# Broadcasting the gain rows and the mLSTM gate maxima by way of DRAM instead of by matmuls

## The chip, the cores and the metric

The kernel runs on one core of a Trainium2 chip. The metric is the device time of one execution in microseconds (us); shown are the median, the lowest and the highest of three runs. A profile is a separate execution, recorded instruction by instruction. TensorE (PE) does the matmuls, VectorE (DVE), ScalarE (ACT) and GpSimd (POOL) the elementwise work. SyncE (SP) issues every DMA of this kernel, from one queue and in order. The granted clock (PEclk) is the share of full speed that TensorE was allowed.

## The reference

Two blocks on 256 tokens of 1024 features in float32. The first block (two layers of feed-forward and a convolution and recurrence mixer) is hardly touched. The second is a two-layer network with adaptive norms, on 256 tokens `x` and 256 context tokens `ctx`. What the change concerns is this:

```python
def adaln(cond, w_mod, b_mod):                      # cond: one vector for x, one for ctx
    m = silu(cond) @ w_mod + b_mod                  # [3 * 1024]
    return split(m, 3)                              # shift, scale, gain "ga"

h = rms_norm(x, g_pre) * (1 + sc) + sh
x = x + ga * rms_norm(mixer(h), g_post)             # layer 0: hyena + attention; layer 1: mLSTM

# mLSTM of layer 1, 8 heads, two directions, chunk form, with running maxima m_row:
s   = (q @ k.T) * exp(d - m_row)                    # d from the cumulated log-gates
num = s @ v + ...; den = sum(s) + ...
h   = num / maximum(abs(den), exp(-m_row))
```

## The kernel before

All float32 products are made of three matmuls of 12-bit halves (`mm3`, L125 to L129). `wload` (L99) brings 1 MB of weights into `raw` (two buffers), and ACT (L96) and DVE (L97) split it into high and low halves `wh`, `wl` (three chunks of buffers). PSUM, the matmuls' output memory, has eight banks: two tagged `mm`, two `tp` (transposes and small products), four `acc`. The program is written as generators that are woven into each other; the tile framework fixes the order on each engine when the kernel is built, and on the chip each engine runs its list strictly in that order.

**The modulation** (`modulation`, L518) makes the vector `silu(cond) @ w_mod` of a layer without matmuls. For each of 24 column blocks a step loads 512 KB of `w_mod` into `mraw` (L534) and DVE multiplies and sums it with the condition, once for `x` and once for `ctx` (L537). So a step has two such DVE operations; of layer 1 the last eight steps have one. Behind the last step the biases are added (L544 to L547). In the Hyena stage of layer 0, `mods` is the modulation of layer 1. There `mraw` has a single buffer (`bufs` is 1), so the load of a step can only start when the DVE operations of the step before are done.

**The Hyena stage** takes 1024 channels in four groups g of 256. `project(g)` does eight groups of 24 matmuls `mm<-HT` (128x512; the text calls them HT groups), each followed by a short convolution on ACT and DVE (L682 to L684). `convolve(g)` transposes the gated input `gg` (L997), multiplies with DFT tables `dft` (`acc<-gT`), takes the product with the filter `F` (DVE, L1015 to L1017), goes back (`acc<-dft,Y`) and gates the result into `hyo`; `rows(g)` multiplies it with output weights. The order in the program is:

```python
mods = modulation(pool, 1, range(12), 1)
weave(hy.project(0), mods, 2)
for g in range(1, 4):
    weave(hy.project(g), paired(chain(hy.convolve(g - 1), *([hy.rows(g - 1)] if g < 3 else [])), mods))
run(mods)
```

`weave` issues a step of `mods` after each two of `project(0)` and then what is left of it, so in the program's text all of `mods` stands ahead of `convolve(0)`; where its instructions land on each engine is the framework's choice.

**The gain rows** (`gain_rows`, L549) put `sqrt(1024) * ga * g_post`, held feature by feature over partitions in `mod`, into a tile `gb` of 1024 columns that is the same on all 128 partitions. Per half, DVE makes a diagonal block `dg` (L553), PE multiplies it by ones (L558) into a `tp` bank, and ACT scales it out (L559). It is called three times, for (layer, condition) = (0,0), (0,1) and (1,0), each shortly ahead of the use of `gb` in `postnorm` (L651).

**The mLSTM.** `mlstm_gates` leaves the running maxima of all heads as `R` [8, 384] per direction and splits them into high and low halves `gRs` (L1113, L1114). `head(h)` needs row h on all 128 partitions: two matmuls with a selector `sel` [8, 128] (L1211, L1220) put it into a `tp` bank; from there DVE adds the mask (`rm`, L1222) and ACT takes the exponentials (L1226). At the end of each head a norm weight `hn` is loaded, broadcast by the DMA (L1252).

Of the kernel before, what the change touches and what calls it, by code (L numbers as in the profile page):

```python
# [9 lines left out]
F32 = mybir.dt.float32  # L10
# [7 lines left out]
P = 128  # L18
D = 1024
# [14 lines left out]
def weave(main, side, n=1):  # L34
    """Issue main, with a step of side after every n steps of it, then what is left of side."""
    side = iter(side)
    for i, _ in enumerate(main):
        if i % n == n - 1:
            next(side, None)
    for _ in side:  # L40
        pass
# [8 lines left out]
def paired(*gens):  # L50
    """The steps of the first, each with one of the others."""
    gens = [iter(g) for g in gens]
    first = gens[0]
    for _ in first:
        for g in gens[1:]:
            next(g, None)
        yield
# [8 lines left out]
def body(ctx: ExitStack, tc: tile.TileContext, a: dict, out: bass.AP):  # L66
# [27 lines left out]
    def split(h, l, src, eng=V):  # L94
        """src = h + l, exactly; h has 12 significant bits, l the other 12."""
        S.copy(h, src)  # L96
        eng.tensor_tensor(l, src, h.bitcast(F32), op=ALU.subtract)  # L97

    def wload(src, parts=1, aside=False):  # L99
        """A [128, 2048] chunk of weights, in two halves (high part, low part)."""  # L100
# [15 lines left out]
    def rsqrt(dst, var, eps, n, scale=1.0):  # L116
        """dst = 1 / sqrt(scale * var + eps)"""
        vv = sp.tile([P, n], F32, tag=f"rs{n}", name="rsv", bufs=2)
        G.tensor_scalar(vv, var, scale, eps, op0=ALU.mult, op1=ALU.add)  # L119
        G.tensor_tensor(dst, vv, mhalf[:, :n], op=ALU.pow)  # L120
# [4 lines left out]
    def mm3(p, lh, ll, rh, rl, first, last):  # L125
        """p += (lh + ll).T @ (rh + rl)"""
# [4 lines left out]
    def agroup(p, w, lhs):  # L131
        """p [128 tok, 512] = sum over kt of lhs(kt).T @ w, w halves of [2 kt x 512]."""
# [7 lines left out]
    def btile(p, w, rhs):  # L140
        """p [128 features, tokens] = sum over kt of w[kt].T @ rhs(kt), w a list of (high, low) [128, 128]."""
        for kt, (wh, wl) in enumerate(w):
            mm3(p, wh, wl, *rhs(kt), kt == 0, kt == len(w) - 1)

    def bcols(w, j):
        """The [128, 128] blocks of feature tile j of a [8 kt x 256] chunk."""
        return [(h[:, k * 256 + j * P :][:, :P], l[:, k * 256 + j * P :][:, :P]) for h, l in w for k in range(4)]

    def rows_acc(chunks, lhs, nch, side=iter(())):
        """Token tiles of [tok, 1024], each in two banks; chunk c of [2 kt x 1024]; the first tile is done early."""  # L150
# [26 lines left out]
    def transposed(blocks):  # L177
        """The transposes of [128, 128] blocks, in one bank."""
# [5 lines left out]
    # ---------------------------------------------------------------- small vectors  # L184
# [14 lines left out]
    def exp_dve(dst, x, t):  # L199
        """exp(x) for x <= 0 by range reduction and a polynomial."""  # L200
# [16 lines left out]
    def softplus_neg(dst, x, t, scale):  # L217
        """dst = scale * log(1 + exp(-x)); log1p(e) as 2 atanh(e / (2 + e))."""
# [19 lines left out]
    # ---------------------------------------------------------------- first block  # L238
    def ln(pool, accs, coef, xa, li):
        """layer_norm(ALPHA x + coef * acc) from acc[column half] of each token tile; the last one is left unscaled."""  # L240
# [40 lines left out]
    def ffn(pool, xt, li, side, w0=None, up=UP):  # L281
        """Chunks of 128 gate and 128 up columns: the first ones token-major, token tile by token tile, as the input
        arrives; the others feature-major."""
# [29 lines left out]
        for j in range(first, 2 * NG):  # L313
            if w0 and j == 0:
                # both column blocks of each part as it arrives, in a bank each
# [17 lines left out]
    def mixer(pool, mp, xt, li, fv, sp4):  # L333
# [11 lines left out]
        def gates(half, brs=(0, 1)):  # L345
            """sigmoid(g_logits + b_merge) of a column half and some branches, token-major"""
# [38 lines left out]
        def recurrence():  # L385
            """The gates of each head and the scan, two heads to a tile."""
# [21 lines left out]
            # with a = exp(-p), u = tanh(p / 2): 1 - a = u (1 + a), so sqrt(1 - a^2) = sqrt(u) (1 + a)  # L408
# [23 lines left out]
        def conv_branch():  # L432
            """columns c0 v0 | b0 c1 | v1 b1 | ..."""
# [83 lines left out]
    # ---------------------------------------------------------------- second block  # L517
    def modulation(pool, l, chunks, bufs):  # L518
        """silu(cond) @ w_mod + b_mod of a layer, feature-major, for some chunks of 256 features."""
# [19 lines left out]
        if 11 in chunks:  # L539
            for v in range(2):  # L540
# [5 lines left out]
                if n == 24:  # L546
                    V.tensor_tensor(m[:, 16:24], m[:, 16:24], fv2[:, l, 4, :], op=ALU.mult)  # L547

    def gain_rows(g, l, v, tmp):  # L549
        """g = sqrt(D) * ga * g_post of (layer, cond) as rows [128 (same), 1024]."""  # L550
        for q in range(2):
            dg = tmp()
            V.tensor_tensor(  # L553
                dg.rearrange("p (f n) -> p f n", f=4), ident.unsqueeze(1).broadcast_to([P, 4, P]),
                mod[:, l, v, 16 + 4 * q : 20 + 4 * q].unsqueeze(2).broadcast_to([P, 4, P]), op=ALU.mult,
            )
            p = psum("tp")
            TE.matmul(p, lhsT=ones, rhs=dg, start=True, stop=True)  # L558
            S.mul(g[:, q * 512 : (q + 1) * 512], p, ROOT)  # L559
# [6 lines left out]
    def row_scale(ss):  # L566
        """1 / sqrt(sum + D eps) of the sums of squares of two halves"""
# [9 lines left out]
    def unit_half(x, h, rs, dst):  # L577
        """dst = half of x * rsqrt(mean(x^2) + eps)"""
        V.tensor_scalar(dst, x[:, HALVES[h]], rs, ROOT, op0=ALU.mult, op1=ALU.mult)

    def prenorm_cols(xns, l, v, ht, tmp):
        """* g_pre * (1 + sc) + sh, feature-major into ht[:, kt, h/l, v*256 + token]."""
# [16 lines left out]
    def prenorm_half(xn, h, t, l, v, ht):  # L599
        """The same for half the features of one token tile, xn overwritten."""  # L600
# [11 lines left out]
    def prenorm_tile(x, t, l, v, ht, js, ss=None):  # L612
        """x [128 tokens, 1024] normed into ht; js: two halves of scratch"""
# [13 lines left out]
    def ctx_start(ht):  # L627
        """The context's part of ht for layer 0."""
# [14 lines left out]
    def postnorm(y, gb, x, js, after, ss=None, eng=V):  # L643
        """x += gb * (y * rsqrt(mean(y^2) + eps)), js: two halves of scratch; after(h) follows each half"""
# [10 lines left out]
    def next_layer(y, gb, x, t, l, v, ht, js):  # L655
        """the end of a layer and the start of the next one, for a token tile"""
# [7 lines left out]
    def out_rows(lhs, chunks, ys, first, toks, bank="acc"):  # L664
        """ys[tok] (+)= lhs(kt, tok).T @ rows of the chunks."""
# [14 lines left out]
    def dwconv(y, p, wv, bv):  # L680
        """3-tap convolution along the tokens of p [128 ch, segments x 256] (zero at each end)."""
# [4 lines left out]
    class Attention:  # L686
# [18 lines left out]
        def tables(s):  # L705
            """rope tables times the norm weights"""
# [11 lines left out]
        def qk(s, p, n, i, tt, dst):  # L718
            """norm and rope of n heads in p [128 tok, n*128]; transposed into dst[:, head, h/l, tok]."""
# [55 lines left out]
        def gate(s, g, h):  # L775
            """silu of the attention gate of one head, times 2"""
# [9 lines left out]
        def softmax(s, sc, e):  # L786
            """e = softmax of the scores sc [128 q, keys]"""
# [63 lines left out]
    def dft_tables(pool, n, raw):  # L851
        """cos, sin (and with n = 4 the weighted ones of the way back), high and low parts."""
# [10 lines left out]
    def hyena_filter(pool):  # L863
        """The long filter's transform, 256 channels at a time, to DRAM; 1 / its sum of magnitudes into il1."""
# [8 lines left out]
        def sine(p, b, nm):  # L873
            """sin(freq * (p + b)) of [64, 256]"""
# [69 lines left out]
    class Hyena:  # L944
# [10 lines left out]
        def project(s, g):  # L955
            """projections, short convolutions and gate of 256 channels; transposes of the convolution's input"""
# [34 lines left out]
        def turn(s, g, segs, gT):  # L991
            """the convolution's input, token-major"""
# [7 lines left out]
        def forward(s, n, gT, Y, bank="acc"):  # L1000
            """transform and product with the filter, n segments"""
# [19 lines left out]
        def back(s, g, segs, Y, hy):  # L1021
            """back from the transform; gate"""
# [20 lines left out]
        def convolve(s, g):  # L1043
            """transform, product with the filter, back; gate"""
# [14 lines left out]
    def mlstm_gates(ht, keep, tmp, gws, res):  # L1059
        """The gates' tables, one per direction, into res; tmp(i, n) gives [128, n] of scratch i."""  # L1060
# [24 lines left out]
        for d in range(2):  # L1085
# [15 lines left out]
            # carried maxima before X2, A, B  # L1101
# [5 lines left out]
            # running maxima of the queries of A, of B less the sum of A's log-gates, of B  # L1107
# [5 lines left out]
            Rs = keep.tile([8, 2, 384], F32R, tag=f"gRs{d}", name="gRs")  # L1113
            split(Rs[:, 0, :], Rs[:, 1, :], R.rearrange("p a n -> p (a n)"))  # L1114
# [14 lines left out]
            res.append((Rs, kb, (X1, X2, A, B)))  # L1129
            yield  # L1130

    class Mlstm:
# [19 lines left out]
        def gate(s, h, bank="mm"):  # L1152
            """output gates of a head, token-major: tanh(o / 2) and 2 silu(z)"""
# [11 lines left out]
        def project(s, h):  # L1165
# [20 lines left out]
            if h % 2 == 0:  # L1186
                # values of two heads, with a column of ones for the denominator
# [14 lines left out]
        def head(s, h):  # L1202
# [8 lines left out]
            sel = s.pool.tile([8, P], F32R, tag="sel", name="sel", bufs=2)  # L1211
            V.tensor_copy(sel, ident[:8, h : h + 1].broadcast_to([8, P]))
# [3 lines left out]
            for d in range(2):  # L1216
                Rs, kb, (X1, X2, A, B) = s.gates[d]
                pr = psum("tp")[:, :384]
                for i in range(2):
                    TE.matmul(pr, lhsT=sel, rhs=Rs[:, i, :], start=i == 0, stop=i == 1)  # L1220
                rm = s.pool.tile([P, 384], F32, tag="rm", name="rm", bufs=1)
                V.tensor_tensor(rm, pr, s.msk[:, d, :], op=ALU.add)  # L1222
                # weights, transposed: key tiles X1, X2, A for the queries of A, B; then B for B
# [42 lines left out]
        def finish(s):  # L1266
            """the last head's output, feature-major"""
# [11 lines left out]
        def last(s, gb, xa, after):  # L1279
            """the last two heads' part of the output, and the end"""  # L1280
# [35 lines left out]
    # ---------------------------------------------------------------- the two blocks  # L1316
# [66 lines left out]
    with new_pool("ys") as pys:  # L1383
# [12 lines left out]
        with new_pool("ph") as pool:  # L1396
# [8 lines left out]
            # the last channels by segment, so that the next layer's start runs beside the context's part  # L1405
            gb = pool.tile([P, D], F32, tag="mraw", name="gb", bufs=1)
            gain_rows(gb, 0, 0, lambda: flat(hy.t2("dg")))
# [21 lines left out]
            gain_rows(gb, 0, 1, lambda: flat(hy.t2("dg")))  # L1429
# [9 lines left out]
    with new_pool("yo") as pys, new_pool("pm") as pool:  # L1439
# [24 lines left out]
        gain_rows(gb, 1, 0, lambda: pool.tile([P, 512], F32, tag="kc", name="dg", bufs=1))  # L1464
# [3 lines left out]
def _layout(np, i):  # L1468
    """Rearranges the inputs for the loads; values and types stay."""
# [50 lines left out]
    # second block  # L1520
# [31 lines left out]
    # constants of the shapes  # L1552
# [44 lines left out]
```

## Time and profile before

| what | value |
|---|---|
| time, median of 3 runs | 2193.03 us (2190.1 to 2194.29) |
| span of the profiled execution, a run of its own | 2195.8 us |
| PE busy | 2136.7 us, 97% of the span |
| PE weight loads (PEld) busy | 1870.8 us, 85% |
| DVE busy | 1604.1 us, 73% |
| ACT busy | 1081.0 us, 49% |
| moved by DMA | 361.93 MB, mean 165 GB/s |

The span is the profiled execution's own time: nothing lies around it in the record. It is 2.8 us above the median and 1.5 us above the slowest of the three runs. PE's share is an average; where a stretch shows PE busy all the time, only PE's own work or an added PE wait moves the end, and where it shows gaps, something else ends last. A busy PE isn't yet a PE at its peak, because matmuls overlap: the distance from one start to the next says what one costs.

### The profile page before, as it was taken

The numbers are of one execution on the slowest core, as the hardware profiler recorded it, in microseconds if no ns is written. First come the engines' busy times: TensorE is split into PE (matmuls) and PEld (weight loads), VectorE is DVE, ScalarE is ACT, GpSimd is POOL, SyncE is SP. The second block draws the span as 40 slices with busy tenths as digits, with TensorE's granted clock in tenths as the row PEclk, the third lists the DMA queues.
The fourth block names the chain that finished last, engine by engine and source line by source line (L and its number), as shares of the span: only waits on it lengthen the run. The fifth ranks groups of instructions, "written<-read, shape, count | busy, mean of one in ns | idle before, by whom it ended". The sixth has DMA issues, their size and how long they took to land.

```text
span 2195.8 us, 32522 instructions
## 1 busy us (share of the span) xinstructions
PE 2136.7 (97%) x12986; PEld 1870.8 (85%) x12986; DVE 1604.1 (73%) x2616; ACT 1081.0 (49%) x1655; POOL 143.2 (7%) x137
## 2 busy tenths in 40 slices
PE   8999999999999999999999999999999989999998
PEld 8988897889989987988889977888888877788886
DVE  7665777689977656776676568756898796875766
ACT  5554566544435444575455444544333354654654
POOL 0000221000000001220010022000000012000001
PEclk9999999999999999999999999999999999999999
DMA  8554654567765555546555543104444223233231
GB/s 290 196 182 148 214 180 170 199 238 261 282 222 211 185 185 174 195 156 216 192 192 192 185 148 116 66 31 176 150 163 168 76 92 128 80 104 134 99 138 59
DMA packets 62688, 361.93 MB, mean 165 GB/s; under 512 B 7591, under 2 KB 10696, under 8 KB 25032
## 3 DMA queue, kind: packets, MB, share of 16 engines
q1 hardware_dynamic: 62536, 359.85, 46.6%
q8 instruction: 102, 1.67, 0.3%
q14 instruction: 50, 0.41, 0.1%
HBM read 356.68 MB, written 3.15 MB: 164 GB/s over the span
## 4 chain that ended last, share of the span: by engine, by line
PE 82%; DVE 8%; ACT 4%; issue 2%; POOL 2%; DMA 1%; SPq 0%; DVEq 0%; POOLq 0%; ACTq 0%
PE mm L127 14%; PE mm L128 14%; PE mm L129 14%; PE acc L129 12%; PE acc L128 12%; PE acc L127 12%; DVE wl L97 3%; DMA raw<-in_w 1%; PE tp L181 1%; ACT wh L96 1%; DVE v L255 1%; DVE bst L256 1%; PE tp L127 1%; POOL rsv L119 0%; PE tp L128 0%
## 5 line engine op out<-in xcount | busy, mean ns | idle before, releaser
L97 DVE TENSOR_TENSOR wl<-raw,wh 128x1024 fp32r<-128x1024 f32 (+1 forms) x566 | 707.4, 1259 | 274.2 <-ACT wh L96 268.1
L96 ACT CAST wh<-raw 128x1024 fp32r<-128x1024 f32 (+1 forms) x590 | 607.2, 1046 | 474.7 <-PE acc L129 163.8
L127 PE MATMUL mm<-xT,wh 128*128 128x256 f32 x1048 | 294.3, 281 | 7.2 <-ACT wh L96 7.2
L129 PE MATMUL mm<-xT,wl 128*128 128x256 f32 x1048 | 294.4, 281 | 2.7 <-POOL wl L97 2.7
L128 PE MATMUL mm<-xT,wh 128*128 128x256 f32 x1048 | 293.9, 280 | 0.0
L129 PE MATMUL acc<-xT,wl 128*128 128x256 f32 x856 | 239.9, 280 | 2.1 <-DVE u L423 0.9
L127 PE MATMUL acc<-xT,wh 128*128 128x256 f32 x856 | 239.6, 280 | 0.4 <-ACT wh L96 0.4
L128 PE MATMUL acc<-xT,wh 128*128 128x256 f32 x856 | 239.5, 280 | 0.0
L127 PEld LDWEIGHTS mm<-xT,wh 128*128 128x128 f32 x1048 | 198.1, 189 | 8.0 <-ACT wh L96 7.4
L129 PEld LDWEIGHTS mm<-xT,wl 128*128 128x128 f32 x1048 | 197.9, 189 | 3.3 <-POOL wl L97 3.2
L128 PEld LDWEIGHTS mm<-xT,wh 128*128 128x128 f32 x1048 | 198.2, 189 | 0.2
L127 PE MATMUL mm<-HT,wh 128*128 128x512 f32 (+1 forms) x448 | 171.5, 383 | 0.9 <-DVE vv L97 0.9
L128 PE MATMUL mm<-HT,wh 128*128 128x512 f32 (+1 forms) x448 | 170.3, 380 | 0.0
L129 PE MATMUL mm<-HT,wl 128*128 128x512 f32 (+1 forms) x448 | 170.3, 380 | 0.0
L129 PEld LDWEIGHTS acc<-xT,wl 128*128 128x128 f32 x856 | 161.1, 188 | 2.9 <-DVE u L423 1.4
L127 PEld LDWEIGHTS acc<-xT,wh 128*128 128x128 f32 x856 | 161.2, 188 | 0.6 <-ACT wh L96 0.6
L128 PEld LDWEIGHTS acc<-xT,wh 128*128 128x128 f32 x856 | 161.4, 189 | 0.0
L129 PE MATMUL acc<-wh,ht 128*128 128x512 f32 x352 | 139.4, 396 | 0.0
L127 PE MATMUL acc<-wh,ht 128*128 128x512 f32 x352 | 139.4, 396 | 0.0
L128 PE MATMUL acc<-wl,ht 128*128 128x512 f32 x352 | 139.3, 396 | 0.0
L127 PE MATMUL mm<-wh,HT 128*128 128x512 f32 x288 | 114.8, 399 | 0.8 <-DVE dn L1244 0.8
L128 PE MATMUL mm<-wl,HT 128*128 128x512 f32 x288 | 113.8, 395 | 0.0
(494 smaller groups left out, 4421.7 us busy)
## 6 DMA issues: line engine op xcount, KB each, us to landing
raw<-in_w SPq DMA_DIRECT2D x131, 1024.0 KB, 4.8
raw<-in_wi_cvb SPq DMA_DIRECT2D x24, 1024.0 KB, 4.8
mraw<-in_w_mod SPq DMA_DIRECT2D x48, 512.0 KB, 4.2
raw<-in_wi_g SPq DMA_DIRECT2D x16, 1024.0 KB, 4.7
raw<-in_e_hy SPq DMA_DIRECT2D x16, 1024.0 KB, 4.9
raw<-in_o_oz SPq DMA_DIRECT2D x16, 1024.0 KB, 4.8
raw<-in_e_out SPq DMA_DIRECT2D x10, 1024.0 KB, 4.7
raw<-in_wi_r SPq DMA_DIRECT2D x8, 1024.0 KB, 4.7
```

Source lines behind the costliest of these rows:

```text
L96: S.copy(h, src)
L97: eng.tensor_tensor(l, src, h.bitcast(F32), op=ALU.subtract)
L127: TE.matmul(p, lhsT=lh, rhs=rh, start=first, stop=False)
L128: TE.matmul(p, lhsT=lh, rhs=rl, start=False, stop=False)
L129: TE.matmul(p, lhsT=ll, rhs=rh, start=False, stop=last)
L181: TE.transpose(tp[:, i * P : (i + 1) * P], b, ident)
L255: V.scalar_tensor_tensor(v[:, c], acc[h], coef, xa[t][:, c], op0=ALU.mult, op1=ALU.add)
L256: V.bn_stats(st[:, h, :], v[:, c])
```

## The change

The gain goes out to DRAM at the end of `modulation`: `gain_out` transposes eight columns of `mod` on PE into a `tp` bank, ACT scales them, and a DMA stores 8 x 128 numbers. `gain_rows` is then one DMA that reads those 4 KB for each of 128 partitions. In the mLSTM, `R` is stored to DRAM as it is (no split), and each head reads its row, once per direction, for all partitions into an SBUF tile `pr` with two buffers, from which the mask's sum and the exponentials (L1222 and L1226; in the new file L1226 and L1230) read. Other lines of the diff only drop comments.

```diff
@@ modulation, behind the adds
                 if n == 24:
                     V.tensor_tensor(m[:, 16:24], m[:, 16:24], fv2[:, l, 4, :], op=ALU.mult)
+                    gain_out(pool, l, v)
+
+    gdram = {(l, v): dp.tile([KT, P], F32, tag=f"gd{l}{v}", name=f"gd{l}{v}") for l, v in ((0, 0), (0, 1), (1, 0))}
+
+    def gain_out(pool, l, v):
+        tp = psum("tp")
+        TE.transpose(tp[:KT, :P], mod[:, l, v, 16:24], ident)
+        r = pool.tile([P, 512], F32, tag="cjunk", name="gr")[:KT, :P]
+        S.mul(r, tp[:KT, :P], ROOT)
+        nc.sync.dma_start(gdram[l, v], r)
 
-    def gain_rows(g, l, v, tmp):
-        for q in range(2):
-            dg = tmp()
-            V.tensor_tensor(
...
-            p = psum("tp")
-            TE.matmul(p, lhsT=ones, rhs=dg, start=True, stop=True)
-            S.mul(g[:, q * 512 : (q + 1) * 512], p, ROOT)
+    def gain_rows(g, l, v):
+        nc.sync.dma_start(g, gdram[l, v].rearrange("f n -> (f n)").partition_broadcast(P))
@@ mlstm_gates
-            Rs = keep.tile([8, 2, 384], F32R, tag=f"gRs{d}", name="gRs")
-            split(Rs[:, 0, :], Rs[:, 1, :], R.rearrange("p a n -> p (a n)"))
+            Rd = dp.tile([8, 384], F32, tag=f"gRd{d}", name="gRd")
+            nc.sync.dma_start(Rd, R.rearrange("p a n -> p (a n)"))
@@ Mlstm.head
-            sel = s.pool.tile([8, P], F32R, tag="sel", name="sel", bufs=2)
-            V.tensor_copy(sel, ident[:8, h : h + 1].broadcast_to([8, P]))
+            prs = []
+            for Rd, _, _ in s.gates:
+                pr = s.pool.tile([P, 384], F32, tag="pr", name="pr", bufs=2)
+                nc.sync.dma_start(pr, Rd[h].partition_broadcast(P))
+                prs.append(pr)
...
-                pr = psum("tp")[:, :384]
-                for i in range(2):
-                    TE.matmul(pr, lhsT=sel, rhs=Rs[:, i, :], start=i == 0, stop=i == 1)
+                pr = prs[d]
```

The new transposes also change the order of the engines in the Hyena stage. The lists below are the order fixed at the build, line, operation, output from inputs and shape; the new file's lines are some three further down.

PE before, in the Hyena stage, where `convolve(0)` begins: nine HT groups (216 matmuls) stand ahead of its transposes `tp<-ident,gg`, and the tenth right behind them.

```order
L128 MATMUL mm<-HT,wh 128x512
L129 MATMUL mm<-HT,wl 128x512
L997 MATMUL tp<-ident,gg 128x128 x8
L127 MATMUL mm<-HT,wh 128x512
L128 MATMUL mm<-HT,wh 128x512
```

PE now, at the same place: 18 HT groups (432 matmuls) stand ahead, then the gain's transpose L555, which reads `mod`, and only then `convolve(0)`.

```order
L128 MATMUL mm<-HT,wh 128x512
L129 MATMUL mm<-HT,wl 128x512
L555 MATMUL tp<-ident,mod 8x128
L1000 MATMUL tp<-ident,gg 128x128 x8
L127 MATMUL acc<-gT,dft_15115 128x512 x2
L128 MATMUL acc<-gT,dft_15115 128x512
L129 MATMUL acc<-gT,dft_15116 128x512
```

Nine HT groups moved ahead of `convolve(0)`, and behind L555 no HT group stands until `rows(0)` is done.

DVE before, at the same place in the program: short convolutions (`cv`), the convolution's input (`gT`), weight splits (`wl`) and steps of the modulation (L537) alternate.

```order
L683 SCALAR_TENSOR_TENSOR cv_15536<-mm,fvc,cv_15536 128x2x255
L97 TENSOR_TENSOR gT<-tp,gT 128x512
L684 SCALAR_TENSOR_TENSOR cv_15536<-mm,fvc,cv_15536 128x2x255
L97 TENSOR_TENSOR gT<-tp,gT 128x512
L537 ISA cjunk,mod<-mraw,cb 128x1024
L537 ISA mod 128x1
L97 TENSOR_TENSOR wl<-raw,wh 128x1024
```

DVE now, behind the last short convolution of the 18 HT groups: the 13th step and the head of the 14th, with one chunk's splits between.

```order
L686 SCALAR_TENSOR_TENSOR cv_16046<-mm,fvc,cv_16046 128x2x255
L687 SCALAR_TENSOR_TENSOR cv_16046<-mm,fvc,cv_16046 128x2x255
L537 ISA cjunk,mod<-mraw,cb 128x1024
L537 ISA mod 128x1
L537 ISA cjunk,mod<-mraw,cb 128x1024
L537 ISA mod 128x1
L97 TENSOR_TENSOR wl<-raw,wh 128x1024 x2
L537 ISA cjunk,mod<-mraw,cb 128x1024
```

DVE now, where that ends: the last step, the adds, and the convolution's input.

```order
L537 ISA cjunk,mod<-mraw,cb 128x1024
L537 ISA mod 128x1
L544 TENSOR_TENSOR mod<-mod,fv_81 128x24
L545 SCALAR_TENSOR_TENSOR mod<-mod,fv_81 128x8
L547 TENSOR_TENSOR mod<-mod,fv_81 128x8
L97 TENSOR_TENSOR gT<-tp,gT 128x512 x2
L1018 TENSOR_TENSOR pr<-acc,F 128x512
```

From `cv_16046` to L544 stand 16 of the operations L537: four steps with two and eight with one, with nothing of the convolution between. All 24 steps now stand ahead of `gT`; before, the last was well behind `convolve(0)`.

SP before, at the last loads of the modulation: they stand between loads of weights and of the filter `F`.

```order
L104 DMA raw<-in_e_hy 128x2048
L534 DMA mraw<-in_w_mod 128x1024 x4
L989 DMA F<-fd_88 128x1024
L534 DMA mraw<-in_w_mod 128x1024
L104 DMA raw<-in_e_hy 128x2048
```

SP now: the last ten stand in a row, followed by the gain's read and store.

```order
L104 DMA raw<-in_e_hy 128x2048
L534 DMA mraw<-in_w_mod 128x1024 x10
L562 DMA gb<-gd_86 128x1024
L558 DMA gd_88<-gr 8x128
L992 DMA F<-fd_90 128x1024
L104 DMA raw<-in_e_hy 128x2048
```

The filter load behind them is that of `convolve(1)`; `convolve(0)` has its own far ahead.

## Rows read from the trace of the kernel before

**Rows 1.** Windows: stretch, PE, PEld, DVE, ACT, POOL busy (instructions), clock, DMA share, GB/s.

```profile
1560.00:1600.00 40.00, 40.00 (x198) 33.23 (x198) 36.87 (x57) 11.79 (x17) 0.00 (x0) 1.00 0.39 138
2000.00:2040.00 40.00, 40.00 (x192) 32.78 (x191) 22.52 (x34) 20.20 (x32) 0.00 (x0) 1.00 0.45 157
```

**Rows 2.** PE's timeline at the ninth HT group: start, duration, instruction.

```profile
1560.05 0.39 PE L127 MATMUL mm<-HT,wh 128*128 128x512 f32 x1
...
1564.03 0.39 PE L129 MATMUL mm<-HT,wl 128*128 128x512 f32 x1
1564.27 1.04 PE L997 MATMUL tp<-ident,gg 128*128 128x128 f32 x8
```

**Rows 3.** DVE's timeline at the first steps of the modulation in the Hyena stage.

```profile
1548.51 0.08 DVE L537 DVE_READ_ACCUMULATOR2_ANT mod<- 128x1 f32 x1
...
1551.75 1.23 DVE L537 CUSTOM_DVE_ANT_0 cjunk<-mraw,cb 128x1024 bf16<-128x1024 f32 x1 [0.58 <-DMA mraw<-in_w_mod]
...
1553.02 1.23 DVE L537 CUSTOM_DVE_ANT_0 cjunk<-mraw,cb 128x1024 bf16<-128x1024 f32 x1
...
1562.57 0.08 DVE L537 DVE_READ_ACCUMULATOR2_ANT mod<- 128x1 f32 x1
...
1565.28 0.75 DVE L683 SCALAR_TENSOR_TENSOR cv<-mm,fvc,cv 128x510 f32<-128x510 f32 x1 [2.02 <-ACT cv L682]
```

**Rows 4.** The tile `mraw`: its loads, from issue to landing.

```profile
DMA to landing us min/median/max: 3.0/4.2/7.7
```

**Rows 5.** DVE's timeline inside `convolve(0)`.

```profile
1578.41 0.68 DVE L1015 TENSOR_TENSOR pr<-acc,F 128x512 f32<-128x512 f32 x1
1579.01 0.68 DVE L1016 TENSOR_TENSOR pr<-acc,F 128x512 f32<-128x512 f32 x1
```

**Rows 6.** Windows around the only long pause of PE in the Hyena stage.

```profile
1782.00:1786.00 4.00, 0.35 (x4) 0.15 (x1) 4.00 (x9) 3.63 (x9) 1.43 (x2) 1.00 0.00 0
1786.00:1790.00 4.00, 1.78 (x7) 1.52 (x8) 3.15 (x8) 1.13 (x3) 2.53 (x3) 0.55 0.00 0
```

**Rows 7.** PE's groups: busy us, mean ns of one, idle before.

```profile
L1220 PE MATMUL tp<-gRs,sel 8*128 8x384 f32 x32 | 10.1, 388 | 0.0
L558 PE MATMUL tp<-dg,ones 128*128 128x512 f32 x12 | 6.0, 591 | 0.0
```

**Rows 8.** PE's timeline around one pair of selector matmuls.

```profile
1977.04 0.39 PE L129 MATMUL acc<-wh,oT 128*128 128x512 f32 x1
1977.36 0.61 PE L1220 MATMUL tp<-gRs,sel 8*128 8x384 f32 x2
...
1978.13 0.28 PE L128 MATMUL mm<-HT,wh 128*128 128x256 f32 x1
```

**Rows 9.** PE's timeline around one pair of gain matmuls.

```profile
2173.80 1.02 PE L558 MATMUL tp<-dg,ones 128*128 128x512 f32 x2
2174.26 0.80 PE L129 MATMUL mm<-wh,oT 128*128 128x512 f32 x1
2174.89 0.40 PE L127 MATMUL mm<-wh,oT 128*128 128x512 f32 x1
```

**Rows 10.** DMA issues: count, KB each, median us from issue to landing.

```profile
fd<-F SPq DMA_DIRECT2D x8, 256.0 KB, 2.7
hn<-in_o_head_norm SPq DMA_DIRECT2D x8, 128.0 KB, 3.1
```

**Rows 11.** DVE's timeline at head 0: the maxima done, and their first use.

```profile
1880.36 0.27 DVE L1111 TENSOR_SCALAR scr<-scr 8x128 f32<-8x128 f32 x1
...
1886.20 0.54 DVE L1222 TENSOR_TENSOR rm<-tp,msk 128x384 f32<-128x384 f32 x1
```

**Rows 12.** SP's waits, 1880 to 2195: total us, times, longest.

```profile
SPq L1252 <- DVE hs L1262: 99.9, 7, 20.4
```

**Rows 13.** DVE's timeline at the end: last reader of `S`, first of `gb`.

```profile
2163.33 0.28 DVE L1231 SCALAR_TENSOR_TENSOR e<-e,S 128x128 f32<-128x128 f32 x1
...
2185.30 1.41 DVE L651 SCALAR_TENSOR_TENSOR j<-yo,rs,gb 128x512 f32<-128x512 f32 x2 [0.45 <-POOL rs L571]
```

More of the change, by code (lines that the diff above doesn't have):

```diff
@@ L547, in modulation @@
                     V.tensor_tensor(m[:, 16:24], m[:, 16:24], fv2[:, l, 4, :], op=ALU.mult)
-    def gain_rows(g, l, v, tmp):
-        for q in range(2):
-            dg = tmp()
-            V.tensor_tensor(
-                dg.rearrange("p (f n) -> p f n", f=4), ident.unsqueeze(1).broadcast_to([P, 4, P]),
-                mod[:, l, v, 16 + 4 * q : 20 + 4 * q].unsqueeze(2).broadcast_to([P, 4, P]), op=ALU.mult,
-            )
-            p = psum("tp")
-            TE.matmul(p, lhsT=ones, rhs=dg, start=True, stop=True)
-            S.mul(g[:, q * 512 : (q + 1) * 512], p, ROOT)
+                    gain_out(pool, l, v)
[8 more added lines that the diff above has]
+        nc.sync.dma_start(g, gdram[l, v].rearrange("f n -> (f n)").partition_broadcast(P))
     HALVES = [slice(h * 512, (h + 1) * 512) for h in range(2)]
@@ L1128, in mlstm_gates @@
             S.activation(kb[:, 4:6, :], kb[:, 4:6, :], AF.Exp, scale=-1.0)
-            res.append((Rs, kb, (X1, X2, A, B)))
+            res.append((Rd, kb, (X1, X2, A, B)))
             yield
@@ L1216, in head @@
             for d in range(2):
-                Rs, kb, (X1, X2, A, B) = s.gates[d]
-                pr = psum("tp")[:, :384]
-                for i in range(2):
-                    TE.matmul(pr, lhsT=sel, rhs=Rs[:, i, :], start=i == 0, stop=i == 1)
+                _, kb, (X1, X2, A, B) = s.gates[d]
+                pr = prs[d]
                 rm = s.pool.tile([P, 384], F32, tag="rm", name="rm", bufs=1)
@@ L1406, in body @@
             gb = pool.tile([P, D], F32, tag="mraw", name="gb", bufs=1)
-            gain_rows(gb, 0, 0, lambda: flat(hy.t2("dg")))
+            gain_rows(gb, 0, 0)
             hy.filt(3)
@@ L1428, in body @@
             gb = pool.tile([P, D], F32, tag="F", name="gb", bufs=1)
-            gain_rows(gb, 0, 1, lambda: flat(hy.t2("dg")))
+            gain_rows(gb, 0, 1)
             run(hy.rows(3, "mm", range(2, 4)))
@@ L1463, in body @@
         gb = pool.tile([P, D], F32, tag="S", name="gb", bufs=1)
-        gain_rows(gb, 1, 0, lambda: pool.tile([P, 512], F32, tag="kc", name="dg", bufs=1))
+        gain_rows(gb, 1, 0)
         ml.last(gb, xa, lambda t, h: nc.sync.dma_start(out[tsl(t), HALVES[h]], xa[t][:, HALVES[h]]))
```

## The prediction

> **What bounds the kernel now.** I read the windows first. In the Hyena stage, around the place that the change reorders, PE is busy in every microsecond at the full clock while DVE is busy for 36.87 of 40 us, and in the mLSTM PE is busy throughout as well [rows 1]. PE's own work sets the end in both, so a matmul taken out there is time won and a wait put in is time lost. Next I read DVE's timeline for the pace of the modulation, because the new order lets PE wait for its end, then PE's timeline around the removed matmuls for what a pair really costs, and last the DMA issues and SP's waits for what the new transfers take and who stands behind them.
>
> **The gain's transpose: a new wait.** In the new order PE runs 18 HT groups, then the transpose of `mod`, then `convolve(0)`. The transpose needs the last step of the modulation. PE works its list in order, so `convolve(0)` and everything behind it stand behind that wait. Three times have to be worked out: when PE gets there, when `mod` is done, and what PE then finds.
>
> When PE gets there: up to the end of the ninth HT group both orders are the same. The last matmuls of it start at 1564.03, and the 17 before took 3.98 us, so 0.234 us each; a group of 24 takes 5.6 [rows 2]. Nine more take 50.7 us. PE is at the transpose at about 1564.3 + 50.7 = 1615.
>
> When `mod` is done: by 1562.65 five of the 24 steps are through [rows 3]. From the end of a step (1548.51 + 0.08) to the first DVE operation of the next (1551.75) pass 3.16 us, the single buffer's load, and DVE sat idle for the last 0.58 of it; the two operations of a step then take 2.5 us (1551.75 to 1553.02, and 1.23). A step with nothing else in its way takes 5.7 us, and the two last steps, with weight loads and splits between, took (1562.65 - 1548.59)/2 = 7.0 [rows 3]. Steps 6 to 12 take 40 to 49 us, until 1603 to 1612. Step 13 stands on DVE behind the short convolution of the 17th group: that group is off PE at 1564.3 + 8 x 5.63 = 1609.3, its first DVE operation comes 1.0 us later by the ninth group's (1565.28 against 1564.27) [rows 2, 3], and two of them take 1.4, so step 13 starts at about 1612. From there, on DVE nothing but the modulation and a chunk's two splits: step 13 takes 2.5, steps 14 to 16 take 5.7 each with the splits (2 x 1.2) hidden in part, say 19 to 22 us in all, until 1633. Eight steps with one operation follow, each 3.16 + 1.3 = 4.5, so 36 us, and the adds 0.4: `mod` is done at about 1670. The wait is 1670 - 1615 = **55 us**. Bounds: if the loads were hidden (which one buffer excludes, unless a load lands in no time) only DVE's 10 + 8 x 1.3 would be left after 1612, and the wait would be 20; if the steps 6 to 16 go at their best and PE gets its weights late, 46; if each of the last 11 loads took the median of all, 4.2 [rows 4], instead of some 3.0, it would be 67.
>
> What PE then finds: before, the HT groups filled the waits inside `convolve(0)`. They are used up, so it runs bare. Its own PE work is 8 transposes, 24 matmuls of 512 and 48 of 256 columns, 0.8 + 5.6 + 5.6 = 12 us. Bare, its chain is: transposes 1, the two splits of `gT` 1.3, the first six products 1.4, 16 DVE operations from `pr` to `Y` at 0.60 apart 9.6 [rows 5], the way back's last products 2, the gating's four operations on ACT and DVE 2.4, so 18 us; and PE comes out of a long pause. The one pause of that size before, 1782 to 1786, was followed by a granted clock of 0.55, the lower level (1.2 of 2.4 GHz) [rows 6]; four to six us at it add 3 to 5. So about 22 - 12 = **10 us** more, bounds 4 (chain 16, clock at once) and 14. The second transposes of the next convolution come late behind the row sums, by my estimate **2** (0 to 5). HT groups are left for the later convolutions, 14 of the 23 that stood behind the ninth group before, enough to fill those.
>
> The other side of this edit, `gb` as one read of 512 KB, costs nothing on PE: at (0,0) it is issued at once when `mraw` is free, and used 100 us later. At (1,0) it waits for `S`, free at 2163.6, and is needed at 2185.3 [rows 13]; 22 us cover any load shown. The transposes and their copies themselves: three times 0.2 us, **0.5**. DVE's six diagonal blocks and ACT's copies go from engines that aren't the bound there. The first two transposes lie in the first block, where a store of 4 KB behind `w2` loads holds nobody up.
>
> **The matmuls that go.** 32 selector matmuls in 16 pairs: around one, the stream's next place after 1977.04 + 0.234 would be 1977.27, and the matmul at 1978.13 stands second of its stream (256 columns, half of 0.234 each), so the pair cost 1978.13 - 0.12 - 1977.27 = 0.74 us [rows 8], and 16 cost 11.8. Six pairs for the gains: 2174.89 - 2173.80 less one matmul's 0.23 is 0.86 [rows 9], in all 5.2. Together **-17.0 us**; their busy time, 10.1 + 6.0 = 16.1 [rows 7], agrees. The lower bound of the gain is half of it, if PE is not what ends last at some of the places (one gain pair lies in the tail, one near PE's pause).
>
> A rule of the Trainium skill speaks for less: the page "Perfetto Trace Analysis", section "Identifying the Most-Contended Engine", says that matmul busy time is a bad measure, because matmuls are pipelined, and the share of the weight loads a better one. By it the 44 removed matmuls would count by their weight loads, 0.17 us each (191 in 32.78 us [rows 1]), some 7.5 us, and the time would come out 9.5 us higher; it is the last rival below. The spacing of the starts around a pair [rows 8, 9] already leaves the overlap out, so I stay with the 17.0.
>
> **The maxima by DRAM.** What is lost is the way in: a store (2.7, the row of 256 KB) and a broadcast read (3.1, the row of 128 KB) [rows 10] in place of a split and a matmul. At head 0 the maxima are done at 1880.6 and used at 1886.2 [rows 11]: 1880.6 + 5.8 and an issue of each gives 1887, so about **1 us** for both directions (0 to 5: a weight load stands between store and read on SP). For the other heads the rows lie in DRAM and are read when `pr` is free. The reads stand ahead of gate weights on SP, but SP today waits up to 20.4 us for the buffer of `hn` in that queue [rows 12] and PE stays busy, so I count the reads of heads 1 to 7 at nothing; if that cover were gone, each odd head could wait some 4 to 8 us.
>
> **Sum.** 55 + 10 + 2 + 0.5 - 17 + 1 = +51.5 us. On the profiled span, 2195.8, that is 2247; the median of the runs is 2.8 us lower, so I say 2244.5.
>
> **Rivals.**
> *The modulation's loads cost nothing and the rest is won.* If the steps ran at DVE's pace, the wait would be 20 us, and with `convolve(0)` no dearer than before, 20 + 0.5 - 17 + 1 = +4.5; with the few us that DVE gains in `convolve(0)`, now free of L537, 2190 to 2197. For it: the transfers are short and the DMA queues half empty (share 0.39). Against it: one buffer, and 3.16 us between two steps with DVE idle at the end [rows 3].
> *The transpose doesn't gate `convolve(0)`.* This is the case on the other side: the gain would go out beside the convolution, as the place of `gain_rows` in the program before would suggest, and PE would not pause in the Hyena stage. Then the matmuls' 17 us are all that shows, less the 1.5 of the other terms: 2177. It decides as soon as the pause is under some 16 us. For it: `gT` needs nothing of `mod`, and DVE had the convolution's work between the steps before [rows 3]. Against it: the list of PE has the transpose first, and DVE's list all 24 steps ahead of `gT`.
> *The reads block SP in the mLSTM.* `pr` has two buffers, so the reads of a head wait until the head before has used its own; behind them stand gate weights and output weights. With PE late by 4 to 8 us at three or four heads, +16 to +30 on top of the sum: 2260 to 2275. For it: SP runs in order and 16 reads are added. Against it: the waits for `hn`, just as long, cost PE nothing [rows 12].
> *The clock costs more.* If after 55 us of pause the low clock lasted as it does in 1786 to 1790 [rows 6] over all of `convolve(0)` and `rows(0)`, 10 us more: 2255.
> *The removed matmuls were worth less.* If the stream around the pairs had slack, because weight loads are what PE is short of (32.78 of 40 us, [rows 1]), only 7.5 of the 17 us come back: 2254. For it: PE's records overlap. Against it: the stream's next start was late by the whole 0.74 [rows 8].
>
> **Chances.** The forecast (a wait of 46 to 67 us) 0.65, own range 2229 to 2262; the loads hidden 0.06; no gating 0.04; SP blocked 0.12; a dearer clock 0.06; matmuls worth less 0.07. Two in ten are left out, with 2218 below (a wait of some 30) and 2272 above. A measurement of this kernel tells 0.2% (4 us) from no change. The first rival gives 0.02 each to faster and same and the rest to slower, the second 0.04 to faster: faster 0.06, same 0.02, slower 0.92.
>
> **What would show it.** In the profile after: one pause of PE of about 55 us in the Hyena stage, ended by DVE's adds of `mod` through the transpose; the granted clock near 0.55 right behind it; on DVE eight steps at 4.5 us with idle time ended by `mraw`'s load; a bare `convolve(0)` of about 22 us; from the mLSTM's start to its end some 10 us less than before. I am wrong if that pause is under 40 us, if the steps come closer than 4 us, or if PE waits in the mLSTM for `pr` or for weights.

## The result, and the profile after

The changed kernel took 2258.43 us (median of 4 runs, 2247.91 to 2261.36) against 2193.66 (2190.1 to 2202.29, 4 runs). The ratio is 1.0276, 95% interval 1.025 to 1.0303: slower by some 61 us (the two medians differ by 64.8, inside that interval). The forecast was 2244.5, range 2218 to 2272. The profiled execution after has a span of 2246.0 us, 50.2 more than before.

PE's waits, all of the run, kernel after (total us, times, longest):

```profile
PE tp L555 <- DVE mod L547: 54.3, 1, 54.3
PE acc L127 <- ACT Y L96: 7.1, 5, 4.8
PE mm L127 <- ACT wh L96: 5.7, 1, 5.7
...
PE acc L127 <- ACT wt L96: 3.6, 1, 3.6
```

The first line is the pause that the forecast put at 55 us; before, the longest wait of PE in the Hyena stage and behind it was 4.5. The fourth line is new as well, and lies in the mLSTM.

Windows of the kernel after, to be held against [rows 1, 6] (columns as there):

```profile
1600.00:1620.00 20.00, 5.84 (x24) 4.44 (x24) 10.96 (x16) 2.10 (x2) 0.00 (x0) 0.75 0.41 149
1640.00:1660.00 20.00, 0.00 (x0) 0.00 (x0) 5.09 (x9) 0.00 (x0) 0.00 (x0) 0.50 0.30 111
1661.00:1665.00 4.00, 3.38 (x13) 2.88 (x14) 1.83 (x7) 1.44 (x3) 0.00 (x0) 0.55 0.38 132
1665.00:1669.00 4.00, 4.00 (x19) 3.25 (x19) 2.63 (x5) 0.00 (x0) 0.00 (x0) 1.00 0.00 0
1677.00:1681.00 4.00, 4.00 (x21) 4.00 (x20) 0.13 (x1) 0.45 (x1) 0.00 (x0) 0.50 0.03 10
1688.00:1692.00 4.00, 4.00 (x19) 3.23 (x18) 3.62 (x6) 0.00 (x0) 0.00 (x0) 1.00 0.00 0
```

PE's HT groups end inside the first window. In the second it is empty while DVE is busy a quarter of the time. Behind the pause the granted clock is 0.55 for the first 4 us, then 1.00, then down to 0.50 once more, and 1.00 again in the last window. What DVE does meanwhile, kernel after (start, duration, instruction, idle time before it and what ended it), against [rows 3]:

```profile
1627.21 1.22 DVE L537 CUSTOM_DVE_ANT_0 cjunk<-mraw,cb 128x1024 bf16<-128x1024 f32 x1 [3.14 <-DMA mraw<-in_w_mod]
...
1632.22 1.23 DVE L537 CUSTOM_DVE_ANT_0 cjunk<-mraw,cb 128x1024 bf16<-128x1024 f32 x1 [3.78 <-DMA mraw<-in_w_mod]
...
1636.60 1.23 DVE L537 CUSTOM_DVE_ANT_0 cjunk<-mraw,cb 128x1024 bf16<-128x1024 f32 x1 [3.14 <-DMA mraw<-in_w_mod]
...
1659.84 1.23 DVE L537 CUSTOM_DVE_ANT_0 cjunk<-mraw,cb 128x1024 bf16<-128x1024 f32 x1 [3.12 <-DMA mraw<-in_w_mod]
...
1661.41 0.16 DVE L547 TENSOR_TENSOR mod<-mod,fv 128x8 f32<-128x8 f32 x1
```

Each of the eight last steps is 1.2 us of work and 3.1 to 3.8 us of waiting for the one buffer's load: 4.4 to 5.1 us a step (the first two: 1627.21 to 1632.22 to 1636.60). PE comes out of it so (kernel after, PE's timeline):

```profile
1661.62 0.38 PE L555 MATMUL tp<-ident,mod 128*8 128x128 f32 x1 [54.31 <-DVE mod L547]
1661.79 1.91 PE L1000 MATMUL tp<-ident,gg 128*128 128x128 f32 x8
...
1676.84 0.41 PE L128 MATMUL acc<-dft,Y 128*128 128x256 f32 x1
1677.05 0.41 PE L127 MATMUL acc<-dft,Y 128*128 128x256 f32 x1
...
1683.88 0.50 PE L127 MATMUL acc<-wh,hyo 128*128 128x512 f32 x1
```

The eight transposes take 1.91 us where they took 1.04 [rows 2]. The low clock comes a second time inside `convolve(0)`, which now has small waits of 0.4 to 0.8 us: 256 columns every 0.21 us (1676.84 to 1677.05) instead of 0.117. From the transpose to the first product of `rows(0)` it is 22.3 us, for 12 us of PE's work.

To see where the time went, each profile is cut at three starts: the first L537 of the Hyena stage (DVE), the first `qc<-mm` of the mLSTM and the last `oT<-tp` (ACT). All lengths in us:

| kernel | first block and attention | Hyena | mLSTM | tail |
|---|---|---|---|---|
| before | 1532.3 | 303.7 | 343.1 | 16.8 |
| after | 1521.3 | 374.7 | 332.9 | 17.1 |
| late_gain | 1533.8 | 307.2 | 333.0 | 17.1 |
| late_gain_only | 1530.4 | 305.9 | 341.1 | 16.7 |
| mlstm_only | 1528.4 | 306.3 | 334.8 | 16.8 |
| gain_only_in_place | 1524.3 | 377.9 | 341.1 | 16.7 |
| double_select | 1529.0 | 304.8 | 351.8 | 16.8 |
| mixed | 1533.8 | 307.5 | 329.5 | 17.1 |

The other rows are experiments, told below. The first column scatters by 12 us among kernels whose code is the same there up to two small transposes; the profile after happened to be at the short end, so its span hides 11 of the us that Hyena and mLSTM show: +71.0 - 10.2 = +60.8, which agrees with the times. The Hyena column scatters too, by 2.6 us among the three kernels with the code of before there (before, mlstm_only, double_select).

### The profile page after: what moved, and what is told of

Same layout as the page of the kernel before. It is cut to its first block, busy times and chain, and to the rows that moved or that the text cites. A ratio compares the mean times of both kernels' runs of the same rounds, so it can differ in the third digit from the quotient of the medians.

```text
span 2246.0 us, 32477 instructions
## 1 busy us (share of the span) xinstructions
PE 2123.2 (95%) x12945; PEld 1862.8 (83%) x12945; DVE 1598.2 (71%) x2600; ACT 1076.2 (48%) x1650; POOL 147.5 (7%) x137
## 4 chain that ended last, share of the span: by engine, by line
PE 73%; DVE 11%; ACT 5%; DMA 4%; issue 3%; POOL 2%; SPq 0%; DVEq 0%; POOLq 0%; ACTq 0%
PE mm L127 12%; PE mm L128 12%; PE mm L129 12%; PE acc L129 11%; PE acc L127 11%; PE acc L128 11%; DVE wl L97 4%; ACT wh L96 2%; DMA mraw<-in_w_mod 1%; DMA raw<-in_w 1%; DMA raw<-in_wi_cvb 1%; PE tp L181 1%; DVE cjunk L537 1%; POOL HT L97 1%; PE tp L127 1%
## 5 line engine op out<-in xcount | busy, mean ns | idle before, releaser
L537 DVE CUSTOM_DVE_ANT_0 cjunk<-mraw,cb 128x1024 bf16<-128x1024 f32 x88 | 107.3, 1220 | 41.8 <-DMA mraw<-in_w_mod 41.3
```

The source lines that it names most:

```text
L537: V.tensor_tensor_reduce(junk, raw, cb[:, v, :], 1.0, 0.0, op0=ALU.mult, op1=ALU.add, accum_out=m)
```

## The experiments

Theory: the order (PE's list has the gain's transpose, and so the whole modulation, ahead of `convolve(0)`) is the loss; the removed matmuls are worth 17 us. Rivals: the reads from DRAM cost time; the removed matmuls are worth less. The kernel before ran beside these kernels on the same chip, at 2197.46 us (29 runs, first four) and 2197.13 (19 runs, last four).

**late_gain.** The gain of layer 1 goes out later:

```diff
                 if n == 24:
...
-                    gain_out(pool, l, v)
+                    if l == 0:
+                        gain_out(pool, l, v)
...
             run(mods)
+            gain_out(pool, 1, 0)
```

> The changed kernel with one edit: the gain of layer 1 is transposed and stored after the loop over the channel groups, not at the end of the modulation. The order on PE is then as before again, nine HT groups ahead of convolve(0). Theory (the 54 us pause at the transpose and the bare convolve(0) behind it are the whole loss; the removed matmuls are worth 17 us): 2193.7 - 17 + 1.5 = 2178, range 2173 to 2184, no pause over 5 us on PE in the Hyena stage. Rival 1 (the reads from DRAM cost time in themselves, in the mLSTM or through the queue of SP): 2195 to 2210. Rival 2 (the removed matmuls count by their weight loads, 7.5 us): 2188.

Measured 2189.55 us, ratio 0.9969 (0.9956 to 0.9983). The pause is gone, and 67 (by the ratios) to 69 us (by the medians) with it. PE's waits in the Hyena stage, kernel late_gain:

```profile
PE acc L127 <- ACT Y L96: 5.1, 2, 4.8
PE tp L181 <- DVE j L583: 4.4, 3, 3.0
PE acc L129 <- POOL HT L97: 3.1, 1, 3.1
```

So the order was the loss. But the gain over before is 6.8 us (3.7 to 9.7) and not 15.5: of the time, rival 2 was nearer. The next two say which part is short.

**late_gain_only** has the edit of late_gain, and the mLSTM as before (the diff's mLSTM part undone); **mlstm_only** has that part alone.

> Only the gain rows by way of DRAM, the gain of layer 1 stored late as in late_gain; the mLSTM with its selector matmuls as before. Theory: six pairs at 0.86 us go, 0.5 us of transposes come: 2193.7 - 4.7 = 2189. Rival 2: about 2192. Rival 1, if the gain's reads cost: 2196 or more.

Measured 2196.95 us, 1.0004 (0.9991 to 1.0017): the gains by DRAM are worth nothing, where 4.7 us were expected. The expectation was counted from 2193.7, and the kernel before took 2197.46 beside this one; against that, no change lies closest to rival 2 (some 2 us faster).

> Only the mLSTM's maxima by way of DRAM; the gain rows by matmuls as before. Theory: 16 pairs at 0.74 us go, 1 us of lateness at head 0 comes: 2193.7 - 10.8 = 2183. Rival 2 (weight loads alone, 5.5 us of the 7.5): 2189. Rival 1 (the reads hold up SP and PE waits for weights): 2194 to 2215.

Measured 2188.9 us, 0.997 (0.9954 to 0.9987): 6.6 us faster, where 10.8 were expected and rival 2 said 5; all that late_gain wins is here. PE's waits in the mLSTM of mlstm_only:

```profile
PE acc L127 <- ACT wt L96: 3.6, 1, 3.6
PE mm L127 <- ACT oT L96: 0.7, 1, 0.7
```

The longest of them stands here on PE's timeline, in the second direction of head 0:

```profile
1899.02 0.58 PE L127 MATMUL acc<-vt,wt 128*128 128x258 f32 x1 [3.64 <-ACT wt L96]
```

SP's timeline of the same kernel ahead of it, the store and the reads:

```profile
1888.42 0.29 SPq L1114 DMA_DIRECT2D gRd<-scr  x1
1889.82 0.80 SPq L1214 DMA_DIRECT2D pr<-gRd  x2
```

Windows around the landing and behind PE's wait, mlstm_only (columns as in [rows 1]):

```profile
1892.00:1893.00 1.00, 1.00 (x8) 0.89 (x7) 0.79 (x1) 0.00 (x0) 0.00 (x0) 1.00 0.68 164
1893.00:1894.00 1.00, 1.00 (x9) 0.96 (x8) 0.00 (x0) 0.84 (x1) 0.00 (x0) 1.00 0.03 9
1899.00:1902.20 3.20, 3.18 (x10) 2.71 (x11) 2.81 (x5) 3.20 (x8) 0.00 (x0) 0.50 0.34 131
```

And the first uses of what was read, on ACT's and on DVE's timeline:

```profile
1893.15 1.05 ACT L96 CAST wh<-raw 128x1024 fp32r<-128x1024 f32 x1 [1.49 <-PE mm L128]
...
1894.78 0.90 ACT L1227 ACTIVATE e<-pr,gkb 128x256 f32<-128x256 f32 x2
1895.45 0.55 DVE L1223 TENSOR_TENSOR rm<-pr,msk 128x384 f32<-128x384 f32 x1
```

The store is issued at 1888.42 and the reads behind it from 1889.82 on. The DMA engines are busy until 1893 and all but idle after it, so the rows have landed by then, some 4.8 us behind the store's issue. Their first use is ACT's at 1894.78, DVE's at 1895.45; neither waited for the DMA. ACT's list has the cast `wh` ahead of the use, and that waited 1.49 us for a matmul of PE. PE then waits for the weights `wt` made of the rows, and runs at the low clock for 3.2 us behind that wait.

**gain_only_in_place** is the changed kernel with the mLSTM's part undone.

> The gain rows by way of DRAM exactly as in the change, the mLSTM as before. Theory: the whole loss is here, and the mLSTM's gain of 11 us is missing: 2258.4 + 11 = 2269, with a pause of PE of 54 us at the transpose. Rival 1 (a part of the loss comes from the reads in the mLSTM): 2235 to 2255.

Measured 2266.64 us, 1.0331 (1.0304 to 1.0357), 69.7 us above late_gain_only, from which only the place of one `gain_out` (transpose, copy and store) differs. Theory held, and rival 1 fell: without the mLSTM's reads the kernel is 8 us slower than the changed kernel, not faster.

**double_select** prices the pairs. On the kernel before:

```diff
-                for i in range(2):
-                    TE.matmul(pr, lhsT=sel, rhs=Rs[:, i, :], start=i == 0, stop=i == 1)
+                for _ in range(2):
+                    for i in range(2):
+                        TE.matmul(pr, lhsT=sel, rhs=Rs[:, i, :], start=i == 0, stop=i == 1)
```

> The kernel before with each pair of selector matmuls done twice (the second pair starts the bank anew, the result is the same): 16 pairs more, and nothing else. Theory: a pair costs PE 0.74 us where it is the bound, so +11.8 us, 0.54% slower; between the projections of the first head and the last head's output the profile is longer by 11 to 12 us. Rival (they count by their weight loads, 0.17 us each): +5.4 us, 0.25% slower. What it tells: whether the 6.6 us that mlstm_only won instead of 11.8 come from cheaper pairs, or from a price of the reads (its profile shows a wait of 3.64 us at the first head).

Measured 2204.15 us, 1.0035 (1.0021 to 1.0048): 7.7 us more by the ratio (4.6 to 10.5): the interval holds the rival's 5.4 and not the theory's 11.8. PE's timeline around one double pair, against [rows 8]:

```profile
1919.96 0.40 PE L129 MATMUL mm<-wh,HT 128*128 128x512 f32 x1
1920.29 0.96 PE L1221 MATMUL tp<-gRs,sel 8*128 8x384 f32 x4
1921.18 0.50 PE L127 MATMUL mm<-wh,HT 128*128 128x512 f32 x1
1921.52 0.39 PE L128 MATMUL mm<-wl,HT 128*128 128x512 f32 x1
```

The stream is late by 1921.52 - 0.23 - (1919.96 + 0.23) = 1.1 us for two pairs and 0.74 for one: a second pair right behind the first adds some 0.35. The other 0.4 is paid once; that it is the price of going over to another stream and back is my reading, which no run separates. So an added pair is not the price of a removed one; the experiment was not the clean test that I took it for.

Its mLSTM is longer by 8.7 us. 16 pairs at 0.35 are 5.6, and 1.1 is a longer wait (1.9 against 0.8 us). Most of the rest is the clock, which was 1.00 in the kernel before at the same place of head 0 (double_select, columns as in [rows 1]):

```profile
1893.60:1897.20 3.60, 3.60 (x16) 3.37 (x16) 1.12 (x4) 1.38 (x3) 0.00 (x0) 0.53 0.00 0
```

PE was busy throughout when its clock fell; 3.6 us at 0.53 lose some 1.7.

**fewer_loads** takes the loads out of the pause:

```diff
-                raw = row()
-                nc.sync.dma_start(raw, a["w_mod"][l, c][:, i * D : (i + 1) * D])
+                if l == 0 or f <= 16:
+                    raw = row()
+                    nc.sync.dma_start(raw, a["w_mod"][l, c][:, i * D : (i + 1) * D])
```

> The changed kernel with the loads of the last seven steps of layer 1's modulation left out: these steps read the block that was loaded before them, so their results are not the reference's; DVE's work is the same. Theory (the pause is paced by one buffer: release, load, DVE): each of the seven steps goes from 4.4 to 5.0 us to 1.3, so 22 to 26 us of the pause of 54 go, and the time falls to about 2234. Rival (the pause is set by DVE's work or by the free bank): no change, 2258.

Measured 2234.27 us, 1.0165 (1.0145 to 1.0186): 24.2 below the changed kernel, where 22 to 26 were expected. Its longest wait of PE:

```profile
PE tp L556 <- DVE mod L548: 30.8, 1, 30.8
```

Two of the steps without a load, on DVE's timeline of fewer_loads:

```profile
1638.30 1.22 DVE L538 CUSTOM_DVE_ANT_0 cjunk<-mraw,cb 128x1024 bf16<-128x1024 f32 x1
1639.57 1.23 DVE L538 CUSTOM_DVE_ANT_0 cjunk<-mraw,cb 128x1024 bf16<-128x1024 f32 x1
```

The pause is 23.5 us shorter, and a step 1.27 us long. The one buffer's loads paced the pause.

**gain_in_acc**: in `gain_out`, `tp = psum("acc" if l else "tp")`.

> The changed kernel with the bank of layer 1's gain transpose taken from the four acc banks instead of the two tp banks. On PE, convolve(0)'s transposes then come ahead of 9 HT groups and the gain's transpose, but its transform still stands behind it. Theory (the place in PE's list decides, whichever bank it is): a pause of 50 to 55 us in front of the transform, 2 to 4 us less behind it as the input is split by then, so 2252 to 2257. Rival (two tp banks are too few, and that makes the wait): 2185 to 2195.

Measured 2258.52 us, 1.0272 (1.0251 to 1.0293): no different from the changed kernel. Its longest wait:

```profile
PE acc L555 <- DVE mod L547: 55.0, 1, 55.0
```

DVE's second split of the convolution's input, and PE 107 us later, kernel gain_in_acc:

```profile
1563.71 0.68 DVE L97 TENSOR_TENSOR gT<-tp,gT 128x512 fp32r<-128x512 f32 x1
1671.56 0.38 PE L555 MATMUL acc<-ident,mod 128*8 128x128 f32 x1 [54.96 <-DVE mod L547]
1671.59 0.77 PE L127 MATMUL acc<-gT,dft 128*128 128x512 f32 x1
```

Which of the two kinds of bank it is doesn't matter; what stands behind the transpose in PE's list does. This run also answers a rival that late_gain leaves open, because late_gain changes DVE's list too: that PE waits because DVE has all 24 steps ahead of `gT`. Here `gT` was ready 107 us before the transform that reads it, and the pause is the same. DVE's products behind the transform still stand behind all 24 steps in this run, so what DVE's list alone would cost without the transpose is not shown. The 2 to 4 us that I expected for the early split of the input didn't show.

**mixed** is late_gain with the selector back for one place, head 0's second direction:

```diff
+            if d == 1:
+                Rs = keep.tile([8, 2, 384], F32R, tag="gRs", name="gRs")
+                split(Rs[:, 0, :], Rs[:, 1, :], R.rearrange("p a n -> p (a n)"))
+                ml_first.append(Rs)
...
-                pr = prs[d]
+                if h == 0 and d == 1:
+                    pr = psum("tp")[:, :384]
+                    for i in range(2):
+                        TE.matmul(pr, lhsT=sel, rhs=ml_first[0][:, i, :], start=i == 0, stop=i == 1)
+                else:
+                    pr = prs[d]
```

> late_gain, and the second direction of the first head gets its maxima by a pair of selector matmuls as before (so its split and one selector come back), all other heads from DRAM. Theory: the 3.64 us that PE waits there go, one pair at 0.74 comes: 3 us less than late_gain, 0.9955 of before, with no wait of PE over 1 us in the mLSTM. Rival (the pairs are worth only 0.35 each and the wait is covered elsewhere): no change against late_gain, 0.997.

Measured 2186.98 us, 0.995 (0.9933 to 0.9968): the fastest of all, 11 us below before. PE's waits in its mLSTM:

```profile
PE mm L127 <- DVE dn L1265: 0.8, 1, 0.8
PE mm L127 <- ACT oT L96: 0.7, 1, 0.7
```

The wait of 3.64 is gone, and the mLSTM is 3.5 us shorter than late_gain's (329.5 against 333.0). The times of the two differ by 2.6 us (4.2 by the ratios), with intervals that overlap, so that step rests on the profiles.

## Why the prediction was right, term by term

**The wait, 55 us: 54.3.** Both its ends came some 3 us later than worked out. Counted from the first L537 of the stage, PE ran out of HT groups after 86 us (1607.3 - 1521.3) and not 82.7, with 2.8 us of waits for short convolutions, which the forecast had at nothing, and `mod` was done after 140 and not 138. The cause, the place in PE's list, is shown by late_gain, by gain_in_acc for the other kind of bank and against DVE's steps ahead of `gT`, and the pace by fewer_loads. The load took 3.1 to 3.8 us a step, not always the 3.16 of [rows 3].

**`convolve(0)` bare, 10 us: 22.3 us against 12 of PE's work, so 10.** The low clock is in it twice, where the forecast had it once; the pause that it took as its model [rows 6] was 4 us long, not "of that size". The price of the place altogether, forecast 55 + 10 + 2 = 67, is 67 to 69 by late_gain and 69.7 by the pair without the mLSTM's part. The 2 for the next convolution was not measured by itself.

**The matmuls, -17 us, and head 0, +1: the sum's wrong step.** The forecast counted 17 - 1 = 16 us to the good; -6.8 was measured (late_gain, with 0.5 for the transposes in it). Three sizes are in this.
- A selector pair at 0.74 us holds for a lone pair that is removed. The cleanest comparison is mixed against late_gain_only, which differ in 15 pairs and the reads in their place: 341.1 - 329.5 = 11.6 us of mLSTM, 0.3 of it in PE's waits, so 0.75 a pair. mlstm_only agrees: its mLSTM is 8.3 us shorter although PE waits some 2 us more in it and runs 3.2 us at the low clock (1.6 lost), which makes 12 for 16 pairs.
- Head 0 costs PE a wait of 3.64 us, with the low clock behind it, and not 1. The forecast took its times from the first direction (1880.6 to 1886.2); the wait is in the second, as mixed shows. The forecast also looked for the cost in the transfers' time. They took 4.8 us where it had 5.8, and the rows lay ready before their first use. So the transfers' time alone does not explain the wait. The order of the engines changed there too: of the matmuls `tp<-qT,kT` that stood between the two directions in the kernel before, none is left there in mlstm_only, so PE comes to the second direction sooner. How the 3.64 divides between this, ACT's order and the transfer stays open.
- The gain pairs of the Hyena stage, 3.4 us, gave nothing. Its length is 305.9 to 307.5 with the gains by DRAM (late_gain_only, late_gain, mixed) and 303.7 to 306.3 with matmuls (before, mlstm_only, double_select). Two windows around the end of the stage suggest why. The kernel before (columns as in [rows 1]):

```profile
1760.00:1780.00 20.00, 19.91 (x111) 16.87 (x110) 18.39 (x39) 10.98 (x24) 1.41 (x5) 1.00 0.16 54
1780.00:1800.00 20.00, 13.05 (x57) 9.35 (x56) 18.75 (x37) 11.98 (x27) 8.00 (x9) 0.83 0.06 17
```

The same windows of late_gain_only:

```profile
1760.00:1780.00 20.00, 18.44 (x98) 14.96 (x98) 18.41 (x39) 11.39 (x25) 0.87 (x2) 1.00 0.15 54
1780.00:1800.00 20.00, 11.50 (x56) 9.22 (x55) 16.19 (x30) 9.29 (x22) 11.50 (x10) 0.83 0.22 79
```

PE is busy 33.0 of these 40 us before and 29.9 here: it has 3 us less to do, and rests 3 us more. A wait of late_gain_only in the Hyena stage that the kernel before has not:

```profile
PE acc L129 <- POOL HT L97: 3.3, 1, 3.3
```

late_gain and mixed have it too (3.1 and 2.4). So PE gave up work there and got a wait for POOL instead; the chain that ends last there runs for the most part over POOL, DVE and ACT. The forecast had left room for this only in a bound ("one near PE's pause").

The rule of the Trainium skill, as the prediction applied it (page "Perfetto Trace Analysis", section "Identifying the Most-Contended Engine") put the removed matmuls at 7.5 us, and with 1.5 of other terms at 6, nearer to the 6.8 measured than my 15.5. The last rival's 2254 was likewise nearer to the 2258.4 measured than the forecast. The profiles show that it came out so for other reasons: the pairs in the mLSTM were worth their spacing, and the rest went into a wait and into a stretch that PE doesn't bound. For a pair added beside another, 0.35 us, two loads of 0.17 came out right.

**The rivals.** The loads were not hidden; the transpose did gate; SP's reads delayed no later head (no wait of PE over 1 us in the mLSTM but head 0's). The low clock did not last over `rows(0)`: it was 1.00 from 1684 to 1692. One of the prediction's own signs of being wrong came true in small: PE did wait in the mLSTM for what is made of `pr`, once, for 3.64 us.

What stays open: the Hyena stage of the kernel before is 1 to 3 us shorter in its one profile than in those of mlstm_only and double_select, whose code is the same there.

## What to carry to other kernels

A small instruction whose input comes late is dear by where it stands in an in-order list: read, in the order that the scheduler made, what is behind it on its engine, and put it where its input is long there. Price removed work by the spacing of the starts around it, but count it only in stretches where that engine never waits. A detour by DRAM cost PE nothing here where the rows were asked for early (heads 1 to 7). At its first use it brought a wait, although the rows landed in time: look at the engines' lists there too, and not only at the transfer's time.

## What the runs showed of the hardware

PE's pace has two levels at the same granted clock. In the first block, where it is busy throughout with matmuls of 256 columns, a stretch of 50 us holds either 426 to 427 of them or 443 to 444. Windows of the kernel after:

```profile
500.00:550.00 50.00, 50.00 (x443) 50.00 (x443) 49.86 (x80) 24.88 (x38) 0.00 (x0) 1.00 0.77 262
900.00:950.00 50.00, 50.00 (x426) 50.00 (x425) 38.16 (x51) 32.39 (x55) 12.05 (x5) 1.00 0.55 191
```

The same windows of the kernel before:

```profile
500.00:550.00 50.00, 50.00 (x427) 50.00 (x426) 47.54 (x76) 22.80 (x35) 0.00 (x0) 1.00 0.74 257
900.00:950.00 50.00, 50.00 (x426) 50.00 (x425) 41.76 (x55) 28.46 (x46) 12.22 (x5) 1.00 0.50 176
```

Of ten profiles, five had the faster pace in 500 to 550, four in 700 to 750, none in 900 to 950. The three that had it in both of the first have the first column of the table at 1521.3, 1524.3 and 1530.4, the four that had it in neither at 1529.0 to 1533.8. It may explain a part of the scatter of the times (12 us within late_gain's runs), though 1530.4 with the faster pace and 1529.0 without it show that it isn't all; what sets it, no run here shows.
